# Seven products for three K pairs in the two output projections of a hybrid decoder trunk

## The chip, the cores and the metric

The kernel runs on one core of one Trainium2 chip. A core has TensorE (PE in the profile, with PEld for the loading of its weights), VectorE (DVE), ScalarE (ACT), GpSimd (POOL) and SyncE (SP, which here only issues DMAs). The metric is the device time of one execution in microseconds; a time is the median of several runs, and a profile is one more execution, taken by itself.

## The reference

The model is a trunk of two layers on 256 tokens of width 2048, in float32. Layer 0 has a Mamba-2 SSD mixer with an inner width of 4096, layer 1 differential attention with 16 heads; each mixer is followed by a SwiGLU FFN of width 5632. Every sub-layer has an RMSNorm before it and one behind it. Cut to what the change touches:

```python
for i in range(DEPTH):                       # DEPTH = 2
    h = rmsnorm(x, norm_mix_pre[i])
    if i % 2 == 0:
        m = ssd_mixer(h, ...)                # ends in: (y normed by group * norm_w) @ w_out   [256,4096]@[4096,2048]
    else:
        m = diff_attention(h, ...)           # ends in: (heads * subln) @ w_out                [256,2048]@[2048,2048]
    x = x + rmsnorm(m, norm_mix_post[i])
    h = rmsnorm(x, norm_ffn_pre[i])
    x = x + rmsnorm(swiglu(h, ...), norm_ffn_post[i])
```

The two products with `w_out` are the output projections of the title. In SSD, `norm_w` is a factor for each of the 4096 inner columns.

## The kernel before

**Products.** The 256 tokens are two tiles t = 0, 1 of 128. Weights stand in HBM as blocks of 128 x 4 x 512: 512 values of K in four rows of 128, and one column of 512 outputs. A block is split into a high part `hi` (ScalarE, rounded to fp32r) and a low part `lo` (VectorE, what is left), in `prep` (L126). The activations are split in the same way. A product of 128 K values is then three matmuls on TensorE, high by high, high by low and low by high, summed in PSUM. Two rows of 128 K values together are called a K pair (`kg` or `kp`).

**`mv`** (L177) makes one column of 512 outputs: for every K pair, 2 token tiles x 2 rows x 3 matmuls, with the second tile's products put off by `lag` steps. **`pair`** (L220) makes two columns of outputs at once. For a K pair that isn't in `seven` it does the same 24 matmuls as `mv` would for both columns. For one in `seven`, the 2 x 2 x 2 block product (token tile, K row, column) is made with seven products instead of eight, from sums of weight blocks (L261 to L263, VectorE) and "forms", sums of activation blocks that `make_form` (L817) prepares once. One more weight sum is made by a DMA that adds while it lands, issued on POOL (L247). Four of the products are summed over all three K pairs in PSUM tiles `cp`, and are combined once, behind the last of the three (L274 to L281). `done` then adds them to the accumulators. The FFNs use `pair` for nearly everything.

**The output projections** are made by `out_proj` (L679). Before the change they use `mv` for all columns. SSD: the first half of K (groups 0 to 3) is multiplied in the middle of the mixer (L786), all four columns; of the second half, column 0 is made at the mixer's end (L788), while its working pools are still open, and columns 1 to 3 after these are closed (L848). `norm_w` is put on the weights: `prep` gets `scale` and works in pieces of 128 x 512 (L137 and L138). Attention: one call, four columns (L1071).

**Behind a projection**, for each token tile: the row's sum of squares (`sums`, ScalarE), the product with the post-norm's row (POOL for columns 0 to 2, VectorE for column 3), then `norm_chain` (L642), which makes x, transposes it on TensorE and writes it, split, to `xT`, the input of the next sub-layer. The rows of the post-norm come from HBM through `pw(n)`, issued on SP; rows 0 and 2 share one buffer, so that row 2's fetch waits for the products with row 0.

**Order.** Work that is to run beside a product is put in a list with `later(k, fn)` and is emitted k steps further on (`tick`, L162), or when a product looks for it (`lookup`). A scheduler then orders the instructions of each engine and of each DMA queue, and places the waits; each engine runs its list in order. Weight blocks have three buffers (`raw`); after the mixer's pools close, `hi` and `lo` have four each.

Of the kernel before, what the change touches and what calls it, by code (L numbers as in the profile page):

```python
# [41 lines left out]
def trunk_kernel(ctx, tc, x_rows, x_cols, vec_cols, vec64, post_rows, lam_rows,  # L42
# [83 lines left out]
    def prep(raw, scale=None):  # L126
        i = seq[0]
        seq[0] += 1
        w = raw.shape[1]
        hi = hl[0].tile([P, w, 512], F32R, tag="hi", name=f"hi{i}")  # L130
        lo = hl[0].tile([P, w, 512], F32R, tag="lo", name=f"lo{i}")
        if scale is None:
            nc.scalar.copy(hi, raw)  # L133
            nc.vector.tensor_tensor(lo, raw, hi.bitcast(F32), op=ALU.subtract)  # L134
        else:
            for j in range(w):
                nc.scalar.activation(hi[:, j], raw[:, j], AF.Copy, scale=scale[j])  # L137
                nc.vector.scalar_tensor_tensor(lo[:, j], raw[:, j], scale[j], hi[:, j].bitcast(F32),  # L138
                                               op0=ALU.mult, op1=ALU.subtract)
        return hi, lo  # L140

    def halves(src, scale=None, raw=None):
# [3 lines left out]
        for e in range(0, 4, w):  # L146
            hi, lo = prep(raw[:, e:e + w], scale and scale[e:e + w])
            for k in range(0, w, 2):
                yield hi[:, k:k + 2], lo[:, k:k + 2]
# [27 lines left out]
    def mv(blocks, stat, evac, lag, scale=None, loaded=()):  # L177
# [14 lines left out]
        for b, src in enumerate(blocks):  # L192
            raw = loaded[b] if b < len(loaded) else None
            sc = scale(2 * b) + scale(2 * b + 1) if scale else None
            for i, (hi, lo) in enumerate(halves(src, sc, raw), 2 * b):
# [24 lines left out]
    def pair(blocks, stat, seven, form, done):  # L220
# [20 lines left out]
        for kp, src in enumerate(blocks):  # L241
# [3 lines left out]
            if kp in seven:  # L245

                nc.gpsimd.dma_start(raw[:, 0:1], src[0][:, 1:2], accum_op=ALU.add)  # L247
            if kp not in seven:
                hi, lo = prep(raw)
                for t in range(NT):  # L250
# [5 lines left out]
                    tick()  # L256
                continue
# [29 lines left out]
    def act_piece(src, name, scale=None):  # L287
# [6 lines left out]
        if scale is None:  # L294
            split(hi, lo, pt)
        else:
            nc.scalar.activation(hi, pt, AF.Copy, scale=scale)
            nc.vector.scalar_tensor_tensor(lo, pt, scale, hi.bitcast(F32), op0=ALU.mult, op1=ALU.subtract)
# [19 lines left out]
    rstd_bc = const.tile([P, S], F32, name="rstd_bc")  # L318

# [295 lines left out]
    def gate_group(g, t):  # L615
# [11 lines left out]
        def piece():  # L627
            ssd_act[(t, g)] = act_piece(yf, f"s{g}_{t}")
        later(4, piece)

# [48 lines left out]
    def out_proj(w, first, last, acts, kgs, step, final, lag, t512, pw, scale=None, ns=range(4), two={}, forms=None, md=None, mid=None):  # L679
# [20 lines left out]
        def row(t, e):  # L700
            if t not in ss4:
                ss4[t] = small.tile([P, 4], F32, tag="ss4", name="ss_m", bufs=3)
            if e not in summed[t]:
                summed[t].add(e)
                return sums(t, e)
# [3 lines left out]
        if last:  # L709
            pw(0)  # L710
            if two:
                pw(1)
        for n, seven in two.items():
            def done(t, c, ps, ss, n=n):
                y, op = ss[(t, c)]
                k = (t, n + 1 - c)
                nc.vector.tensor_tensor(y, ps, y, op=op)
# [6 lines left out]
                else:  # L724
# [3 lines left out]
                 lambda i, j, t: stat(kgs[i], j, t), [kgs.index(kg) for kg in seven], lambda i, f: form_of(lookup(forms, kgs[i]), f), done)  # L728
# [5 lines left out]
        for n in ns:  # L734
# [7 lines left out]
            def evac(t, ps, n=n):  # L742
# [11 lines left out]
                if n == 2:  # L754
                    p3 = small.tile([P, 1], F32, tag="ss1", name="p3", bufs=3)
                    nc.vector.tensor_reduce(p3, ss4[t][:, 0:3], axis=AX.X, op=ALU.add)
                    nc.vector.tensor_scalar(ss4[t][:, 0:1], p3, 1.0 / D, EPS, op0=ALU.mult, op1=ALU.add)
# [4 lines left out]
            mv([w[n, kg // 2] for kg in up[::2]], up_stat, evac, LAG if last and n == 3 else lag,  # L762
               (lambda i: [scale[:, 2 * up[i] + j:2 * up[i] + j + 1] for j in range(2)]) if scale is not None else None)

    for half in range(2):
# [19 lines left out]
        if half == 0:  # L785
            out_proj(w_so, True, False, ssd_act, list(range(8)), 0, False, 1, None, None, ssd_norm)  # L786

    out_proj(w_so, False, False, ssd_act, list(range(8, 16)), 0, False, 1, None, None, ssd_norm, ns=range(0, 1))  # L788
# [28 lines left out]
    def make_form(dct, key, stat, t512, keep=None):  # L817

        xf = t512("xf", (P, NT, 2, P))
        f = t512("f", (P, 4, P))  # L820
        for t in range(NT):
            for j in range(2):
                hi, lo = stat(key, j, t)
                nc.vector.tensor_tensor(xf[:, t, j], hi.bitcast(F32), lo.bitcast(F32), op=ALU.add)
        nc.vector.tensor_tensor(f[:, 0], xf[:, 1, 0], xf[:, 1, 1], op=ALU.subtract)
        nc.vector.tensor_tensor(f[:, 1], xf[:, 1, 0], xf[:, 0, 0], op=ALU.subtract)
        nc.vector.tensor_tensor(f[:, 2], xf[:, 0, 0], f[:, 0], op=ALU.subtract)
        nc.vector.tensor_tensor(f[:, 3], xf[:, 0, 1], f[:, 2], op=ALU.subtract)
        ff = dct[key] = xr_tile("ff", (P, 4, 2, P), F32R)
        split(ff[:, :, 0], ff[:, :, 1], f)  # L830
        if keep:
            nc.sync.dma_start(keep, ff.rearrange("p f h q -> p (f h q)").bitcast(F32))

    def form_of(ff, f):
        return ff[:, f, 0], ff[:, f, 1]

# [11 lines left out]
    out_proj(w_so, False, True, ssd_act, list(range(8, 16)), 0, False, LAG2, t512, load_post(0), ssd_norm, ns=range(1, 4))  # L848
# [285 lines left out]
```

## Time and profile before

| what | value |
|---|---|
| median of three runs | 2540.5 us (2540.33 to 2541.4) |
| the profiled execution's own time | 2541.16 us |
| its span, first to last instruction | 2539.4 us |
| granted TensorE clock, mean | 0.998 |
| weight loads of the SSD projection | 32 of 1024 KB, issued from 252.9 to 670.0 us |
| weight loads of the attention projection | 16 of 1024 KB, issued from 1690.2 to 1788.2 us |
| DMA | 536.16 MB, mean 211 GB/s |

The stretch of the second half of the SSD projection is about 612 to 698 us of the span, that of the attention projection about 1736 to 1816 us. In the page, a group's line gives its source line, engine, operation, tiles and shapes, its count, then its busy time and the mean ns of one, and then the idle time of the engine ahead of them with what ended it. The chain that ended last is followed back from the last instruction through what released each step, and shows which work sets the end. A matmul's recorded duration overlaps the next one's, so the pace of products is read from the start of one to the start of the next.

### The profile page before, as it was taken

Reading aid. Unit: us, or ns where it says so; the run is one execution under the profiler, and the core shown is the slowest. Engines: PE = TensorE matmul, PEld = TensorE weight load, DVE = VectorE, ACT = ScalarE, POOL = GpSimd, SP = SyncE. Lnnn points to the kernel's source line nnn. Section 1 sums busy time; section 2 is a strip of 40 time slices with the busy share of each in tenths; the row PEclk is TensorE's granted clock in tenths of the full one; section 3 lists DMA queues with packets and bytes.
Section 4 is the critical chain, followed back from the end, with each engine's and each line's share of the span. In section 5 each row is a group of like instructions: output and inputs, shape, how many; then the busy total and the mean of one; then the engine's idle time right before and its main releaser. Section 6 shows DMA issues by size and latency. Waiting matters only on the chain.

```text
span 2539.4 us, 31214 instructions
## 1 busy us (share of the span) xinstructions
PE 2517.3 (99%) x11866; PEld 2071.8 (82%) x11866; DVE 1901.7 (75%) x2274; ACT 1364.6 (54%) x1655; POOL 224.4 (9%) x214
## 2 busy tenths in 40 slices
PE   9999999999999999999999999999999999999998
PEld 7877888788888888888888888887888888888886
DVE  6777547777687888977887765566688889878985
ACT  5767546665565454544454654455655454535453
POOL 0121000110110000001001100001100000010002
PEclk9999999999999999999999999999999999999999
DMA  7545555554776776778677544544666966796673
GB/s 279 197 167 183 186 194 199 166 183 171 257 261 211 254 238 210 235 230 244 209 239 243 189 150 166 183 151 156 241 222 201 292 213 214 234 264 207 211 251 146
DMA packets 141366, 536.16 MB, mean 211 GB/s; under 512 B 14176, under 2 KB 30880, under 8 KB 114208
## 3 DMA queue, kind: packets, MB, share of 16 engines
q1 hardware_dynamic: 125584, 502.91, 57.3%
q0 software_dynamic: 15264, 30.94, 6.4%
q8 instruction: 93, 1.52, 0.2%
q14 instruction: 57, 0.47, 0.1%
q10 hardware_dynamic: 368, 0.32, 0.0%
HBM read 516.22 MB, written 17.89 MB: 210 GB/s over the span
## 4 chain that ended last, share of the span: by engine, by line
PE 91%; DVE 3%; issue 2%; ACT 2%; DMA 1%; POOL 0%; SPq 0%; DVEq 0%; ACTq 0%; POOLq 0%
PE acc L238 36%; PE acc L187 35%; PE cp L238 7%; PE acc L212 5%; PE acc L214 2%; DVE lo L134 2%; ACT hi L133 1%; PE sc L1010 1%; PE pt_f L291 1%; PE py L565 1%; DMA mt<-acum_d 1%; PE ptx L658 0%; PE po L1046 0%; PE pc L472 0%; PE pt_s L291 0%
## 5 line engine op out<-in xcount | busy, mean ns | idle before, releaser
L134 DVE TENSOR_TENSOR lo<-raw,hi 128x2048 fp32r<-128x2048 f32 (+2 forms) x451 | 848.2, 1888 | 363.0 <-ACT hi L133 362.2
L133 ACT CAST hi<-raw 128x2048 fp32r<-128x2048 f32 (+2 forms) x451 | 699.9, 1558 | 592.0 <-DVE raw L263 189.2
L238 PE MATMUL acc<-hi,xT 128*128 128x512 f32 x1840 | 589.0, 390 | 0.0
L187 PE MATMUL acc<-hi,xT 128*128 128x512 f32 x1792 | 586.1, 399 | 0.6 <-ACT hi L133 0.5
L238 PEld LDWEIGHTS acc<-hi,xT 128*128 128x128 f32 x1840 | 345.3, 188 | 71.5
L187 PEld LDWEIGHTS acc<-hi,xT 128*128 128x128 f32 x1792 | 335.8, 188 | 74.1 <-issue 4.9
L238 PE MATMUL acc<-lo,xT 128*128 128x512 f32 x920 | 358.1, 389 | 0.0
L187 PE MATMUL acc<-lo,xT 128*128 128x512 f32 x896 | 352.3, 394 | 2.6 <-DVE lo L134 2.6
L133 ACT CAST hi<-rawm 128x2048 fp32r<-128x2048 f32 (+1 forms) x115 | 207.8, 1807 | 173.7 <-DVE rawm L263 108.3
L134 DVE TENSOR_TENSOR lo<-rawm,hi 128x2048 fp32r<-128x2048 f32 (+1 forms) x115 | 248.1, 2157 | 70.2 <-ACT hi L133 66.1
L238 PEld LDWEIGHTS acc<-lo,xT 128*128 128x128 f32 x920 | 172.7, 188 | 35.7
L187 PEld LDWEIGHTS acc<-lo,xT 128*128 128x128 f32 x896 | 169.0, 189 | 40.2 <-DVE lo L134 5.5
L238 PE MATMUL acc<-hi,ah_f 128*128 128x512 f32 x468 | 183.1, 391 | 0.0
L238 PE MATMUL acc<-hi,al_f 128*128 128x512 f32 x468 | 182.2, 389 | 0.0
L238 PE MATMUL acc<-lo,ah_f 128*128 128x512 f32 x468 | 182.1, 389 | 0.0
L212 PE MATMUL acc<-xT,hi 128*128 128x512 f32 x512 | 180.4, 398 | 0.0
L238 PE MATMUL cp<-hi,ff 128*128 128x512 f32 x468 | 156.8, 389 | 0.0
L214 PE MATMUL acc<-xT,lo 128*128 128x256 f32 x512 | 143.0, 280 | 0.0
L138 DVE SCALAR_TENSOR_TENSOR lo<-raw,cols,hi 128x512 fp32r<-128x512 f32 x128 | 92.5, 769 | 56.6 <-ACT hi L137 56.3
L137 ACT ACTIVATE hi<-raw,cols 128x512 fp32r<-128x512 f32 x128 | 84.6, 715 | 59.4 <-PE acc L187 39.3
L212 PEld LDWEIGHTS acc<-xT,hi 128*128 128x128 f32 x512 | 96.1, 188 | 22.8
L238 PEld LDWEIGHTS acc<-hi,al_f 128*128 128x128 f32 x468 | 87.8, 188 | 18.3
(279 smaller groups left out, 3469.9 us busy)
## 6 DMA issues: line engine op xcount, KB each, us to landing
raw<-in_w_zxbc_dram SPq DMA_DIRECT2D x77, 1024.0 KB, 4.8
raw<-in_w_d_dram SPq DMA_DIRECT2D x98, 512.0 KB, 5.8
raw<-in_w_g_dram SPq DMA_DIRECT2D x96, 512.0 KB, 6.0
raw<-in_w_u_dram SPq DMA_DIRECT2D x96, 512.0 KB, 5.8
raw<-in_w_qkv_dram SPq DMA_DIRECT2D x48, 1024.0 KB, 4.7
raw<-in_w_so_dram SPq DMA_DIRECT2D x32, 1024.0 KB, 4.8
rawm<-in_w_g_dram SPq DMA_DIRECT2D x64, 512.0 KB, 5.9
rawm<-in_w_u_dram SPq DMA_DIRECT2D x64, 512.0 KB, 6.0
```

The lines of the kernel that those rows point to most:

```text
L133: nc.scalar.copy(hi, raw)
L134: nc.vector.tensor_tensor(lo, raw, hi.bitcast(F32), op=ALU.subtract)
L137: nc.scalar.activation(hi[:, j], raw[:, j], AF.Copy, scale=scale[j])
L138: nc.vector.scalar_tensor_tensor(lo[:, j], raw[:, j], scale[j], hi[:, j].bitcast(F32), op0=ALU.mult, op1=ALU.subtract)
L187: nc.tensor.matmul(acc[t], a, b[:, j], start=(i == 0 and j == 0 and q == 0), stop=(i == last and j == 1 and q == 2))
L212: nc.tensor.matmul(acc[ct], hi[:, j, cs], x.rearrange("p a s -> p (a s)"), start=(i == 0 and j == 0), stop=False)
L214: nc.tensor.matmul(acc[ct][:, :S], lo[:, j, cs], x[:, 0], start=False, stop=(i == last and j == 1))
L238: nc.tensor.matmul(acc[k], a, b, start=first and q == 0, stop=last and q == 2)
L291: nc.tensor.transpose(pt[:, j], src[:, j * P:(j + 1) * P], ident)
L565: nc.tensor.matmul(py[e * 64:(e + 1) * 64, a], xd[c][:, 2 * a + e], mts[c][:, 2 * a + e], start=True, stop=True)
L1010: nc.tensor.matmul(sc[c][:, h], qT[cp, h % 2, ts], kT[cp, h % 2, :nk * P], start=True, stop=True)
```

## The change

Both projections make columns 1 and 2 with `pair`, and three of its eight K pairs take seven products: K pairs 9, 11 and 13 of the second half in SSD, 1, 3 and 5 in attention. Column 0 and column 3 stay with `mv`. SSD's first half stays as it was, but for the scale.

- `norm_w` is no longer put on the weights. `act_piece` puts it on the activations, as a scale of each of the four 128-wide parts, so that `prep` loses its second branch.
- `make_form` and `form_of` move up, and `make_form` can be told where to put the form (`at`). The forms of the projections are put in `xT` (`idle_xT`), the mixer's input, which has had its last reader by then and isn't written again before `norm_chain`.
- `pair` gets `chip`: the sum that was made by a DMA issued on POOL is made by one more VectorE instruction on the loaded block.
- `pair` also gets `lead`, which stays 0, and its plain K pairs are written as a function; their order is the same.
- Attention's projection becomes two calls: column 0, then columns 1 and 2 with column 3.
- The rows' sums of squares and post-norm products move: row 0 at step 3 of the pair, the fetch of post-norm row 2 at step 4, rows 1 and 2 at steps 4 and 5 behind the pair. The sum over three rows is made when the third is there.
- `attention_group` is cut into functions for values, keys and the rest, called in the same order, and some helpers of `ffn` move out of it.

```diff
-    def prep(raw, scale=None):
+    def prep(raw):
...
-        if scale is None:
-            nc.scalar.copy(hi, raw)
-            nc.vector.tensor_tensor(lo, raw, hi.bitcast(F32), op=ALU.subtract)
-        else:
-            for j in range(w):
-                nc.scalar.activation(hi[:, j], raw[:, j], AF.Copy, scale=scale[j])
-                nc.vector.scalar_tensor_tensor(lo[:, j], raw[:, j], scale[j], hi[:, j].bitcast(F32),
-                                               op0=ALU.mult, op1=ALU.subtract)
+        nc.scalar.copy(hi, raw)
+        nc.vector.tensor_tensor(lo, raw, hi.bitcast(F32), op=ALU.subtract)
...
-    def pair(blocks, stat, seven, form, done):
+    def pair(blocks, stat, seven, form, done, lead=0, chip=False):
...
-            if kp in seven:
-
+            if kp in seven and chip:
+                nc.vector.tensor_tensor(raw[:, 0], raw[:, 0], raw[:, 1], op=ALU.add)
+            elif kp in seven:
                 nc.gpsimd.dma_start(raw[:, 0:1], src[0][:, 1:2], accum_op=ALU.add)
...
+        for sl in (slice(0, 4),) if scale.shape[1] == 1 else [slice(j, j + 1) for j in range(4)]:
+            sc = scale if scale.shape[1] == 1 else scale[:, sl]
+            nc.scalar.activation(hi[:, sl], pt[:, sl], AF.Copy, scale=sc)
+            nc.vector.scalar_tensor_tensor(lo[:, sl], pt[:, sl], sc, hi[:, sl].bitcast(F32),
+                                           op0=ALU.mult, op1=ALU.subtract)
...
+    def idle_xT(i):
+
+        return xT[i // 2][:, :, :, i % 2 * P:(i % 2 + 1) * P]
...
-            ssd_act[(t, g)] = act_piece(yf, f"s{g}_{t}")
+            ssd_act[(t, g)] = act_piece(yf, f"s{g}_{t}", scale=ssd_norm[:, 4 * g:4 * g + 4])
...
+                if len(summed[t]) == 3:
+                    p3 = small.tile([P, 1], F32, tag="ss1", name="p3", bufs=3)
+                    nc.vector.tensor_reduce(p3, ss4[t][:, 0:3], axis=AX.X, op=ALU.add)
+                    nc.vector.tensor_scalar(ss4[t][:, 0:1], p3, 1.0 / D, EPS, op0=ALU.mult, op1=ALU.add)
...
+            if 1 in two:
+
+                later(3, lambda: [row(t, 0) for t in range(NT)])
+                later(4, lambda: pw(2))
         for n, seven in two.items():
             def done(t, c, ps, ss, n=n):
                 y, op = ss[(t, c)]
                 k = (t, n + 1 - c)
+                if first and last:
+                    nc.vector.tensor_tensor(m[k], ps, y, op=op)
+                    return
...
+    sforms = {}
+    for k, kg in enumerate((9, 11, 13)):
+        later(2 + 2 * k, lambda k=k, kg=kg: make_form(
+            sforms, kg, act_stat(ssd_act), lambda name, shape: s2.tile(list(shape), F32, tag="t2", name=name), at=idle_xT(k)))
+    out_proj(w_so, False, False, ssd_act, list(range(8, 16)), 0, False, 1, None, None, ns=range(0, 1))
...
-    out_proj(w_so, False, True, ssd_act, list(range(8, 16)), 0, False, LAG2, t512, load_post(0), ssd_norm, ns=range(1, 4))
+
+    out_proj(w_so, False, True, ssd_act, list(range(8, 16)), 0, False, LAG2, t512, load_post(0), ns=(3,),
+             two={1: (9, 11, 13)}, forms=sforms)
...
-    out_proj(w_ao, True, True, att, list(range(8)), 2, False, LAG2, t512, load_post(2))
+    aforms = {}
+    for k, kg in enumerate((1, 3, 5)):
+        later(3 + 2 * k, lambda k=k, kg=kg: make_form(aforms, kg, act_stat(att), t512, at=idle_xT(k)))
+    out_proj(w_ao, True, False, att, list(range(8)), 2, False, LAG2, t512, None, ns=(0,))
+    out_proj(w_ao, True, True, att, list(range(8)), 2, False, LAG2, t512, load_post(2), ns=(3,),
+             two={1: (1, 3, 5)}, forms=aforms)
```

127 lines of the change are left out of this document (70 added, 57 removed).

## The prediction

> **What bounds the kernel now.** I read the page first: its head, the busy shares, the granted clock and the chain that ended last.
>
> ```profile
> span 2539.4 us, 31214 instructions
> PE 2517.3 (99%) x11866; PEld 2071.8 (82%) x11866; DVE 1901.7 (75%) x2274; ACT 1364.6 (54%) x1655; POOL 224.4 (9%) x214
> PEclk9999999999999999999999999999999999999999
> PE 91%; DVE 3%; issue 2%; ACT 2%; DMA 1%; POOL 0%; SPq 0%; DVEq 0%; ACTq 0%; POOLq 0%
> ```
>
> The reader is to see that TensorE (PE) has work in flight for 2517.3 of 2539.4 us and holds 91% of the chain. The page warns that a busy PE need not run at its peak, so the next views are the waits of PE alone (in all us, times, longest) and then the merged chain in order of time (start, us, what), at the two output projections and inside one FFN pair.
>
> ```profile
> PE acc L187 <- DVE lo L134: 2.6, 5, 1.3
> PE pc L472 <- ACT tk L478: 1.8, 1, 1.8
> PE ptx L658 <- DVE x L652: 1.5, 3, 0.7
> PE pwarm L328 <- POOL ones L317: 1.3, 1, 1.3
> PE px L552 <- DVE xg L460: 0.9, 2, 0.6
> PE ptx L658 <- issue: 0.7, 1, 0.7
> PE acc L187 <- ACT hi L133: 0.5, 1, 0.5
> ```
>
> ```profile
> 624.12 73.49 PE acc L187 x324
> ...
> 852.13 27.88 PE acc L238 x123
> ...
> 1758.99 53.50 PE acc L187 x235
> ```
>
> These are all waits of PE that the view names, 9.3 us in the whole program and none for a weight load. The chain crosses most of the SSD mixer's last projection as one unbroken run of 324 products: 73.49 / 324 = 0.2268 us from one to the next. The attention projection gives 53.50 / 235 = 0.2277, and a run inside a pair that already uses seven products gives 27.88 / 123 = 0.2267. So a product costs 0.2268 us in the form it has now and in the form it will have; the longer duration that the groups of the page show for a single matmul overlaps its neighbour and isn't the price.
>
> Last, the busy time of each engine in the two stretches (columns: length, PE, PEld, DVE, ACT, POOL, clock, DMA share, GB/s).
>
> ```profile
> 601.37:697.62 96.25, 96.25 (x429) 79.27 (x427) 62.17 (x90) 55.63 (x93) 10.63 (x9) 1.00 0.65 235
> 1736.00:1816.00 80.00, 79.30 (x366) 64.67 (x367) 42.66 (x51) 41.05 (x57) 14.83 (x9) 1.00 0.52 178
> ```
>
> PE is never idle in the first stretch and idle for 0.70 us in the second, at the full clock; VectorE (DVE) is busy 65% and 53%. TensorE's count of products sets the time here, and VectorE is the engine with least room behind it.
>
> **What the change removes on the path.** A column of one projection has 8 K pairs x 2 token tiles x 2 halves x 3 terms = 96 products, two columns 192. Three of the eight K pairs now take 7 x 3 = 21 products where they took 24: 5 x 24 + 3 x 21 = 183, so 9 fewer for each projection and 18 in all. 18 x 0.2268 = 4.08 us. Nothing else leaves TensorE, and nothing is added to it: forms and block sums are made on VectorE and ScalarE (ACT).
>
> The Trainium skill, "TensorE: Matmul & The Clock Gate", section "Back-to-back issue gap", gives about 131 ns for such a product in a sustained stream and about 216 ns for the gap of an isolated one. By these the saving would be an estimated 2.4 or 3.9 us; the 0.2268 us of this trace decides against both, and the sum above does not use them.
>
> **What it adds beside the path.** The rows by shape:
>
> ```profile
> L134 DVE TENSOR_TENSOR lo<-raw,hi 128x2048 fp32r<-128x2048 f32 x241 | 551.0, 2294 | 247.6 <-ACT hi L133 246.9
> L134 DVE TENSOR_TENSOR lo<-raw,hi 128x1024 fp32r<-128x1024 f32 x160 | 210.4, 1319 | 96.5 <-ACT hi L133 96.4
> L138 DVE SCALAR_TENSOR_TENSOR lo<-raw,cols,hi 128x512 fp32r<-128x512 f32 x128 | 92.5, 769 | 56.6 <-ACT hi L137 56.3
> L134 DVE TENSOR_TENSOR lo<-raw,hi 128x1536 fp32r<-128x1536 f32 x50 | 87.6, 1752 | 18.9 <-ACT hi L133 18.9
> L261 DVE TENSOR_TENSOR raw<-raw 128x512 f32<-128x512 f32 x50 | 34.5, 690 | 1.3
> L285 DVE TENSOR_TENSOR ff<-f,ff 128x512 fp32r<-128x512 f32 x18 | 12.3, 687 | 2.4 <-ACT ff L284 2.4
> L284 ACT CAST ff<-f 128x512 fp32r<-128x512 f32 x18 | 11.1, 619 | 13.4 <-PE cp L238 10.2 <-issue 3.0 <-DVE f L828 0.2
> L824 DVE TENSOR_TENSOR xf<-ah_f,al_f 128x128 f32<-128x128 f32 x48 | 11.5, 283 | 0.1
> L664 DVE SCALAR_TENSOR_TENSOR xT<-ptx,cols,xT 128x128 fp32r<-128x128 f32 x96 | 27.8, 345 | 5.3 <-ACT xT L663 5.1
> L285 DVE TENSOR_TENSOR al_s<-pt_s,ah_s 128x512 fp32r<-128x512 f32 x16 | 10.9, 683 | 2.2 <-ACT ah_s L284 2.2
> ```
>
> SSD scale: 128 scaled weight pieces at 0.769 become plain ones. In the last projection that frees 64 x 0.769 = 49.2 us of VectorE, and its old first column and fourth column come back as 8 x 1.319 + 4 x 2.294 = 19.7. The scale moves to 16 activation pieces, four 128x128 steps where one 128x512 stood: 4 x 0.345 - 0.683 = 0.7 us more for each, two or three of them in this stretch (2 us). The other projection of SSD only gets lighter, with PE unbroken there already, so it is costed at nothing.
>
> The pair: 5 x 2.294 for the plain K pairs; a seven-product one takes the new add on the chip and three block sums (4 x 0.690), the three-quarter low part (1.752) and the sums' low part (2.294), 6.81 us. Together 11.5 + 20.4 = 31.9. The end of a pair adds four combinations, and eight instructions in `done` replace four evacuations: 8 x 0.69 = 5.5. Three forms at 8 x 0.283 + 0.687 = 2.95 give 8.9. Sum: 62.2 - 49.2 + 19.7 + 2 + 31.9 + 5.5 + 8.9 = 81 us of VectorE in 96.25 - 9 x 0.2268 = 94.2. By busy time it still fits, behind TensorE. In attention the pair replaces 8 x 2.294 = 18.4: 42.7 - 18.4 + 31.9 + 5.5 + 8.9 = 71 in 78. The weight bytes and their number of landings per K pair stay those of the FFN pairs; the add that those give to a transfer is on VectorE here, so no POOL transfer is added.
>
> What can fail is order, not volume. A seven-product pair followed by a plain one, as an FFN pair of the same kernel runs it on VectorE:
>
> ```profile
> 881.61 1.76 DVE L134 TENSOR_TENSOR lo<-raw,hi 128x1536 fp32r<-128x1536 f32 x1 [2.71 <-ACT hi L133]
> 883.40 0.69 DVE L261 TENSOR_TENSOR raw<-raw 128x512 f32<-128x512 f32 x1
> ...
> 887.53 2.29 DVE L134 TENSOR_TENSOR lo<-raw,hi 128x2048 fp32r<-128x2048 f32 x1 [2.11 <-ACT hi L133]
> 889.74 2.29 DVE L134 TENSOR_TENSOR lo<-rawm,hi 128x2048 fp32r<-128x2048 f32 x1
> ```
>
> From 881.61 to 889.74 + 2.29 = 892.03 are 10.4 us, of which 2.11 is a wait for ScalarE that the next plain low part may fill (then 8.3). With the new add it is 11.1 (or 9.0), against (21 + 24) x 0.2268 = 10.2 on TensorE. So VectorE may lose up to 0.9 us in each of three rounds, 2.7 us for each projection, and needs a lead. What lead it has in SSD:
>
> ```profile
> 625.83 7.37 DVE L138 SCALAR_TENSOR_TENSOR lo<-raw,cols,hi 128x512 fp32r<-128x512 f32 x11
> 633.74 0.69 DVE L748 TENSOR_TENSOR m<-m,acc 128x512 f32<-128x512 f32 x1 [0.54 <-PE acc L187]
> ```
>
> Column 0 ends on TensorE at about 633.7, and by 633.2 VectorE has finished eight pieces of column 1, two blocks or 48 x 0.2268 = 10.9 us of products. The forms (8.9), two pieces (1.4) less the lighter column 0 (16 x 0.769 - 8 x 1.319 = 1.8) take 8.5 of it if no idle time of VectorE takes them up: a lead of 2.4 us or more, against up to 2.7 us lost. The two are about even. The lower bound is no stall; the upper is 2.7 - 2.4 = 0.3 plus three waits of a form for its own ScalarE step, 0.62 each, 2.2 us. I take 0.5 us, nearer to the lower end, because VectorE has idle time to give before column 1: the 56.6 us ahead of L138 are 0.44 for each of its 128 pieces, 7 us in the 16 of column 0. In attention VectorE prepares up to four blocks ahead, and I cost the same loss at nothing; if that cover were gone it would be the 2.7 us.
>
> **A wait added.** `pw(2)`, the third post-norm row, is now fetched after the row-0 products on POOL, early in the pair; it is issued on SP, and weight loads of later K pairs stand behind it there, which ScalarE, VectorE and then TensorE wait for.
>
> ```profile
> 648.64 1.29 POOL L688 TENSOR_TENSOR m<-m,wpost 128x512 f32<-128x512 f32 x1 [27.41 <-DMA wpost<-in_post_rows_dram]
> 655.71 3.30 POOL L688 TENSOR_TENSOR m<-m,wpost 128x512 f32<-128x512 f32 x2 [5.78 <-ACT junk L302]
> SPq L806 <- POOL m L688: 28.2, 6, 9.4
> raw<-in_w_d_dram SPq DMA_DIRECT2D x98, 512.0 KB, 5.8
> 633.22 0.33 SPq L123 DMA_DIRECT2D raw<-in_w_so_dram  x1
> 636.45 1.75 SPq L841 DMA_DIRECT2D x<-in_x_rows_dram  x4
> ```
>
> SP already waits like this 28.2 us in all in the program, up to 9.4 at once, and no PE wait above is for a weight load. So zero is taken. The upper bound is in the rivals.
>
> The Trainium skill, "SBUF — State Buffer", section "Who interferes with whom", speaks against moving the sums to VectorE: its instructions with two SBUF inputs keep out a GpSimd instruction that reads SBUF. The trace agrees in kind (1.29 us alone above, a mean of 1.65 in the pair of 3.30); it would make the wait on SP longer, and gives no term of the sum.
>
> **The sum.** -4.08 + 0.5 = -3.6 us. The profiled execution took 2541.16 (span 2539.4), so 2537.6 on its scale; against the median of 2540.5 it is **2536.9 us**. A measurement of this kernel can tell about 0.2%, 5.1 us, from no change, and the whole saving is below that.
>
> **Rivals.**
>
> *VectorE becomes the bound in SSD.* The lead is short by 0.3 us, the forms' three waits are added and no wait of ScalarE is filled, and what is lost in the first round delays the buffers of the next: a loss of 2 to 5 us, so 2538.4 to 2541.4. For it: 81 of 94 us, and a lead nearly used up. Against it: the FFN pairs run at 10.4 against 10.2 with PE unbroken. 15%.
>
> *The SP queue starves the pair: slower than before.* POOL's row-0 products end at about 648.64 + 3.3 = 651.9, since the row they need lands no earlier. K pair 4 is due on TensorE two plain and two seven-product pairs after column 0: 633.7 + 90 x 0.2268 = 654.1. If its load stands behind `pw(2)`, it lands at 651.9 + 5.8 = 657.7; with a high part (1.9, the 2.11 above less its signals) and a low part (2.3) it is ready at 661.9, 7.8 us late, and the time is 2540.5 - 4.1 + 7.8 = 2544.2. If K pair 2 is held too, due at 643.9, it is 18 us late: 2554. The mechanism makes the kernel slower from a loss of 4.08 us, which is K pair 4's load issued after about 648.2. For it: the calls stand in this order in the code. Against it: the trace shows SP with the loads of columns 1 and 2 (the first of column 2 at 633.22) ahead of the fetch of x (636.45), which stands before them in the code. 12%, of which 7 beyond 2545.6.
>
> *The norm chain gains too.* PE's idle time at the ends of the projections:
>
> ```profile
> 690.00:720.00 30.00, 28.80 (x140) 22.84 (x139) 24.98 (x48) 20.08 (x45) 3.08 (x2) 1.00 0.81 285
> ```
>
> 1.2 us here and 0.7 in attention. Rows 1 and 2 are squared earlier now; if that closes both gaps the time is 2540.5 - 4.08 - 1.9 = 2534.5. Against: the last steps before the transposes are the same. 13%.
>
> *It doesn't do what it says:* all loss is placed so that no product is saved on the path. Since PE is unbroken, I see no place for it, and give it no chance beyond the first rival's upper end.
>
> **How the numbers follow.** The forecast has 60% (2535.6 to 2538.4, its own range), the rivals 15, 12 and 13%. The range of 2535.0 to 2542.0 holds the forecast, the VectorE case and the near end of the norm-chain case, and leaves out the rest of that and the SP case. Faster by over 0.2% (under 2535.4) is the norm-chain case, 0.13; slower by over 0.2% (over 2545.6) is the far part of the SP case, 0.07; within 0.2%, 0.80.
>
> **What would show it.** 11848 products on PE; runs in the chain at 0.2268 in both projections; waits of PE for `lo` near the start of the SSD pair show the second term; a PE wait after an SP wait on POOL shows the slow rival. The forecast is wrong if PE idles over 2 us in either pair, or if the product's pace differs.

## The result and the profile after

The changed kernel takes **2562.4 us** (median; 2561.9 to 2562.9) beside 2540.6 us for the kernel before on the same chip. The ratio is 1.0084, with a 95% interval of 1.007 to 1.0098. The forecast was 2536.9 us, with a range up to 2542.0: the direction is wrong, and so is the range.

First the page of the changed kernel: its head, the busy shares, and the chain that ended last by engine.

```profile
span 2560.7 us, 31277 instructions
PE 2523.2 (99%) x11848; PEld 2072.3 (81%) x11848; DVE 1944.9 (76%) x2346; ACT 1366.6 (53%) x1637; POOL 228.4 (9%) x214
PE 64%; DVE 5%; issue 3%; ACT 2%; DMA 1%; POOL 0%; SPq 0%; DVEq 0%; ACTq 0%; POOLq 0%
```

The 18 products are gone (11866 to 11848), and the busy share of PE still reads 99%. But PE's share of the chain fell from 91% to 64%. A share of busy time didn't show the loss; the share of the chain did.

To place it I cut the span at four marks that both traces have: the last gate `zth` of SSD and the first transpose `ptx` of the norm after it, the last `qk` scaling of attention and the first `ptx` after that. Between them lie the tail of the mixer, column 0, the pair and column 3 of each projection. The windows of before, then of after, with a stretch of 20 us in attention's column 0 for each, and a stretch early in the kernel (length; busy time and records of PE, PEld, DVE, ACT and POOL; granted clock; DMA share; GB/s):

```profile
615.94:698.33 82.39, 81.68 (x365) 67.28 (x364) 54.25 (x79) 48.15 (x81) 10.09 (x8) 1.00 0.67 241
1724.42:1815.67 91.25, 90.56 (x416) 72.75 (x415) 49.37 (x67) 46.73 (x75) 14.83 (x9) 1.00 0.48 166
140.00:145.00 5.00, 5.00 (x22) 3.77 (x21) 4.35 (x9) 2.79 (x6) 0.00 (x0) 1.00 0.63 210
...
1750.00:1770.00 20.00, 20.00 (x102) 16.43 (x101) 9.86 (x14) 10.28 (x13) 6.11 (x4) 1.00 0.34 120
```

```profile
618.60:708.94 90.34, 82.10 (x354) 64.56 (x353) 70.21 (x90) 46.71 (x53) 14.49 (x8) 1.00 0.63 220
1735.50:1837.14 101.64, 93.56 (x406) 73.81 (x404) 73.53 (x117) 51.04 (x78) 15.48 (x9) 0.95 0.42 150
140.00:145.00 5.00, 5.00 (x15) 3.61 (x14) 3.18 (x6) 2.35 (x5) 0.00 (x0) 0.68 0.64 208
1760.00:1780.00 20.00, 14.23 (x53) 11.01 (x54) 13.55 (x35) 7.38 (x13) 2.35 (x3) 0.74 0.18 66
```

SSD's projection grew by 7.95 us and attention's by 10.39, where each should have shrunk by 2.04. Together they lost 18.3 + 4.1 = 22.4 us against their products. Ahead of SSD's mark the span is 2.66 us longer (615.94 to 618.60); most of this first appears at 140 us, where this one profile shows a granted clock of 0.68. Five microseconds at 0.68 are an estimated 1.6 us lost. The fifteen other kernels with the scale moved are 0.8 to 1.5 us late at that mark, each in one profile. Everything else differs by 0.3 us: 7.95 + 10.39 + 2.66 + 0.30 = 21.3, the difference of the spans.

The waits of PE (in all us, times, longest) and a piece of VectorE's order in attention (start, us) show who is late:

```profile
PE pt_o L297 <- DVE ob L1096: 4.3, 2, 3.5
PE acc L181 <- DVE lo L133: 4.1, 7, 1.4
...
PE cp L233 <- ACT hi L132: 1.9, 2, 1.2
PE acc L233 <- ACT hi L132: 1.9, 3, 1.0
PE pp L1079 <- DVE e L1069: 1.9, 1, 1.9
```

```profile
1757.77 0.69 DVE L269 TENSOR_TENSOR raw<-raw 128x512 f32<-128x512 f32 x1
1758.37 0.89 DVE L341 TENSOR_TENSOR xf<-ah_o,al_o 128x128 f32<-128x128 f32 x4
...
1761.10 2.29 DVE L133 TENSOR_TENSOR lo<-raw,hi 128x2048 fp32r<-128x2048 f32 x1
1763.31 0.29 DVE L344 TENSOR_TENSOR f<-xf,f 128x128 f32<-128x128 f32 x1
1763.51 0.68 DVE L1094 TENSOR_REDUCE sso<-ob 128x4 f32<-128x512 f32 x1
...
1765.77 0.69 DVE L1096 TENSOR_TENSOR ob<-po,rs_o 128x512 f32<-128x512 f32 x1 [0.90 <-POOL rs_o L93]
1766.38 0.68 DVE L291 TENSOR_TENSOR xT<-f,xT 128x512 fp32r<-128x512 f32 x1
```

PE has no wait of 0.3 us or more for a form's own tile. VectorE works its list in order. In it, work for the pair (block sums L269, form additions L341 and L344, the pair's low part L133) stands between the softmax and the last `ob` steps, which PE waits for. PE had 53 records in 20 us there, at a mean granted clock of 0.74, where before had 102 at 1.00.

In SSD's pair the chain passes over SP as well: the fetch of the third row, which waited for POOL, then a weight load, then VectorE.

```profile
656.75 0.33 SPq L857
...
658.08 7.03 DMA raw<-in_w_so_dram
...
666.71 3.96 DVE lo L133 x2
```

On TensorE the loss in SSD divides like this: from the last product of the gate to the first of the pair are 24.5 us (617.00 to 641.51), where a kernel with plain pairs (e8_plain below) takes 21.6; the pair itself takes 48.4 us, where 183 products at 0.2267 are 41.5. So about 2.9 us go to column 0 and 6.9 to the pair.

### The profile page after: what moved, and what is told of

It reads as the page before. It is cut to its first block, busy times and chain, and to the rows that moved or that the text cites. A ratio compares the mean times of both kernels' runs of the same rounds, so it can differ in the third digit from the quotient of the medians.

```text
span 2560.7 us, 31277 instructions
## 1 busy us (share of the span) xinstructions
PE 2523.2 (99%) x11848; PEld 2072.3 (81%) x11848; DVE 1944.9 (76%) x2346; ACT 1366.6 (53%) x1637; POOL 228.4 (9%) x214
## 4 chain that ended last, share of the span: by engine, by line
PE 64%; DVE 5%; issue 3%; ACT 2%; DMA 1%; POOL 0%; SPq 0%; DVEq 0%; ACTq 0%; POOLq 0%
PE acc L233 35%; PE acc L181 12%; PE cp L233 7%; PE acc L205 5%; DVE lo L133 3%; PE acc L207 2%; ACT hi L132 2%; PE sc L1052 1%; PE pt_f L297 1%; DMA raw<-in_w_d_dram 1%; PE ptx L698 0%; PE po L1088 0%; DVE raw L267 0%; DVE raw L268 0%; DMA raw<-in_w_so_dram 0%
## 5 line engine op out<-in xcount | busy, mean ns | idle before, releaser
L133 DVE TENSOR_TENSOR lo<-raw,hi 128x2048 fp32r<-128x2048 f32 (+2 forms) x509 | 938.4, 1851 | 389.5 <-ACT hi L132 386.0
L132 ACT CAST hi<-raw 128x2048 fp32r<-128x2048 f32 (+2 forms) x509 | 773.2, 1526 | 635.9 <-DVE raw L269 218.5
L133 DVE TENSOR_TENSOR lo<-rawm,hi 128x2048 fp32r<-128x2048 f32 (+1 forms) x115 | 247.6, 2153 | 71.0 <-ACT hi L132 67.1
L233 PEld LDWEIGHTS acc<-hi,al_f 128*128 128x128 f32 x468 | 87.8, 188 | 18.3
L233 PEld LDWEIGHTS cp<-hi,ff 128*128 128x128 f32 x468 | 87.9, 188 | 18.1
L233 PEld LDWEIGHTS acc<-hi,ah_f 128*128 128x128 f32 x468 | 87.9, 188 | 17.9
```

What stands on the lines that cost most here:

```text
L233: nc.tensor.matmul(acc[k], a, b, start=first and q == 0, stop=last and q == 2)
```

## The experiments

The expectations name these theories. **V**: VectorE does the pair's extra work ahead of steps on which PE waits, or makes the pair itself late; later V was split into **F** (the forms do it) and **S** (the block sums and the chain of a seven-product K pair do it). **Q**: SP waits for POOL before it fetches the third row, with weight loads behind it. **O**: a seven-product K pair stands too early in the pair. **P**: VectorE and POOL slow each other. The last two columns are the two stretches marked above, from one profile each; the count of products alone gives 80.35 and 89.21 for three seven-product K pairs. How far one profile can be trusted shows in after, e4_attlate and e2_ssd: VectorE, SP and POOL carry the same list in SSD there, and the stretch took 90.34, 91.54 and 92.30 us. So in a stretch that stalls, a difference under 2 us tells nothing by itself. Stretches with plain products agree within 0.2 us.

| kernel | median us | ratio to before (95%) | SSD | attention |
|---|---|---|---|---|
| before | 2540.6 | 1 | 82.39 | 91.25 |
| after | 2562.4 | 1.0084 (1.0070, 1.0098) | 90.34 | 101.64 |
| e1_scale | 2541.7 | 1.0002 (0.9992, 1.0011) | 82.21 | 91.26 |
| e2_ssd | 2551.1 | 1.0037 (1.0024, 1.0051) | 92.30 | 91.23 |
| e3_row2 | 2559.1 | 1.0073 (1.0056, 1.0089) | 88.18 | 101.15 |
| e4_attlate | 2554.4 | 1.0052 (1.0037, 1.0067) | 91.54 | 94.45 |
| e5_rowpool | 2559.9 | 1.0076 (1.0061, 1.0091) | 90.26 | 101.49 |
| e6_late | 2550.8 | 1.0039 (1.0024, 1.0053) | 85.04 | 95.85 |
| e7_latedma | 2549.8 | 1.0036 (1.0023, 1.0049) | 88.16 | 94.61 |
| e8_plain | 2542.1 | 1.0007 (0.9998, 1.0016) | 82.32 | 91.43 |
| e9_noform | 2546.6 | 1.0025 (1.0015, 1.0034) | 82.71 | 96.25 |
| e10_late_noform | 2542.8 | 1.0008 (0.9998, 1.0017) | 81.85 | 91.83 |
| e11_nosum | 2540.0 | 0.9999 (0.9989, 1.0008) | 80.95 | 90.92 |
| e12_one | 2541.0 | 1.0003 (0.9994, 1.0012) | 81.54 | 91.00 |
| e13_noform_rowpool | 2544.3 | 1.0014 (1.0005, 1.0023) | 80.24 | 96.33 |
| e14_late_noform_sp | 2547.5 | 1.0025 (1.0015, 1.0036) | 82.74 | 95.99 |
| e15_poolform | 2562.2 | 1.0084 (1.0068, 1.0101) | 90.54 | 101.95 |

**e1_scale**: the kernel before, with only the scale of SSD moved from the weight pieces to the activation pieces.

```diff
-            ssd_act[(t, g)] = act_piece(yf, f"s{g}_{t}")
+            ssd_act[(t, g)] = act_piece(yf, f"s{g}_{t}", scale=ssd_norm[:, 4 * g:4 * g + 4])
```

> The kernel before, with only the norm factor moved from the weights to the activation pieces. The prediction's view (TensorE unbroken there): 2540.5 us, within 1. The rival view, from the trace after, where the cores' first stretch ends 2.3 us later from 140 us on with a granted clock of 0.68 in one 5 us stretch: 2542 to 2544 if the small steps of the pieces cause it, 2540.5 if it comes with the rest of the change.

2541.7 beside 2541.2 us in its own batch: the moved scale costs nothing that can be told in the time.

**e2_ssd**: the change without its attention part.

```diff
-    out_proj(w_ao, True, False, att, list(range(8)), 2, False, LAG2, t512, None, ns=(0,))
-    out_proj(w_ao, True, True, att, list(range(8)), 2, False, LAG2, t512, load_post(2), ns=(3,),
-             two={1: (1, 3, 5)}, forms=aforms)
+    out_proj(w_ao, True, True, att, list(range(8)), 2, False, LAG2, t512, load_post(2))
```

> The change without the attention part (its projection by four plain columns). If the two projections lose independently, the trace after puts 10.6 us of loss ahead of the first norm chain, so 2551 us; if the attention part is innocent, 2562.

2551.1, as forecast for two independent losses: about half of the loss belongs to each projection. They can be studied apart.

**e3_row2**: the fetch of the third row issued ten steps later.

```diff
-                later(4, lambda: pw(2))
+                later(14, lambda: pw(2))
```

> The change with the fetch of post-norm row 2 ten steps later, so that no weight load of the pair stands behind a row product of POOL on SP. Theory Q (the SP queue starves the pair): the pairs lose 5.2 us in SSD and 3.7 in attention over what they save, so 2553 to 2557 us. Theory V (VectorE's list: forms and block sums stand ahead of the mixers' last steps): within 1.5 us of 2562.4.

2559.1, between the forecasts of Q and V. In SSD the fetch moved behind five loads and not two, and the stretch is 2.2 us below the shortest of the three above; another 1.9 us lie ahead of the first mark, before any such fetch. In attention SP's order stayed as it was, and the edit didn't test it.

**e4_attlate**: attention's seven-product K pairs at places 2, 4, 6 of the eight, not 1, 3, 5 (counted from 0), and its forms eight steps later.

```diff
-        later(3 + 2 * k, lambda k=k, kg=kg: make_form(aforms, kg, act_stat(att), t512, at=idle_xT(k)))
+        later(11 + 2 * k, lambda k=k, kg=kg: make_form(aforms, kg, act_stat(att), t512, at=idle_xT(k)))
-    out_proj(w_ao, True, True, att, list(range(8)), 2, ...
+    out_proj(w_ao, True, True, att, [0, 2, 1, 4, 3, 6, 5, 7], 2, ...
```

> The change with attention's forms eight steps later, and the seven-product K pairs at places 2, 4, 6 of the pair instead of 1, 3, 5. Theory V: attention's column 0 loses 9.2 us to forms and block sums ahead of the softmax, so about 2553 us. Theory Q: column 0's loss is no matter of the forms, and at most 3.7 us come back, 2558 to 2562.

2554.4, near V's 2553, and attention's stretch is 7.2 us shorter: the loss in its column 0 is one of order, and the instructions are the same. The pair behind it stayed long.

**e5_rowpool**: the third row fetched on POOL's own queue, so that SP doesn't wait.

```diff
-                nc.sync.dma_start(w[n], post_rows[ix, ...
+                (nc.gpsimd if n == 2 else nc.sync).dma_start(w[n], post_rows[ix, ...
```

> The change with every fetch of post-norm row 2 issued on POOL, behind its own row products, so that SP never waits for POOL there (in the runs before, SP waited 21 to 23 us for it beside attention's pair). Theory Q: the late loads are what both pairs lose, so -4 in SSD and -3 or more in attention, 2553 to 2556 us. Theory V: VectorE's chain of high part, low part, sums and low part is what the pairs wait for, so no more than run e3_row2 gave in SSD and nothing in attention, 2558 to 2560.

2559.9, as V had it: neither stretch moves by more than 0.2 us. The wait on POOL is gone from SP's queue in the pair, but beside attention's pair SP now waits up to 20.9 us at once for a low part on VectorE. Of the 2.5 us less than the change took, 1.67 lie ahead of the first mark (616.93 and 618.60), before any such fetch.

**e6_late**: e5_rowpool with the order of e4_attlate in both projections, and SSD's forms made behind column 0 too.

```diff
+        later((1, 4, 8)[k], lambda k=k, kg=kg: make_form(sforms, kg, act_stat(ssd_act), t512, at=idle_xT(k)))
-    out_proj(w_so, False, True, ssd_act, list(range(8, 16)), 0, ...
+    out_proj(w_so, False, True, ssd_act, [8, 10, 9, 12, 11, 14, 13, 15], 0, ...
-        later(3 + 2 * k, ... make_form(aforms, ...
+        later((11, 13, 16)[k], ... make_form(aforms, ...
```

> As e5_rowpool, and both projections make their forms behind column 0, with the seven-product K pairs at places 2, 4, 6. Theory V: the 4.8 us of SSD's column 0 and the 8.5 of attention's come back, and the two plain K pairs ahead give VectorE a lead; what stays is its 11.1 us for each 10.2 of TensorE plus the forms, 5 us in a pair at most: 2543 to 2548. Theory Q alone: as e5_rowpool, less the 8 us that run e4_attlate gave.

2550.8, above V's forecast. Column 0 of SSD takes its old time again (21.6 us on TensorE, 615.67 to 637.29), but both pairs are still long. VectorE's timeline at the first addition of column 0 in the changed kernel, and then in e6_late with a part of its pair:

```profile
641.11 0.68 DVE L800 TENSOR_TENSOR m<-m,acc 128x512 f32<-128x512 f32 x1
```

```profile
634.80 0.68 DVE L800 TENSOR_TENSOR m<-m,acc 128x512 f32<-128x512 f32 x1
...
643.54 4.49 DVE L133 TENSOR_TENSOR lo<-raw,hi 128x2048 fp32r<-128x2048 f32 x2 [1.38 <-ACT hi L132]
647.95 3.07 DVE L341 TENSOR_TENSOR xf<-ah_s,al_s 128x128 f32<-128x128 f32 x4
...
656.02 1.75 DVE L133 TENSOR_TENSOR lo<-raw,hi 128x1536 fp32r<-128x1536 f32 x1
```

From the last gate (618.60, 617.16; before 615.94) to this addition are 22.5, 17.6 and, before, 17.8 us. The changed kernel's VectorE reaches it 4.7 us later than before; TensorE itself lost 2.9 us in column 0. In e6_late about 8 us of forms stand between two low parts, and the four additions that take 0.89 us elsewhere took 3.07 beside a row product on POOL. In the whole stretch of SSD these are the waits of PE for the pair, both for a form itself:

```profile
PE acc L233 <- ACT xT L290: 2.2, 1, 2.2
...
PE acc L233 <- DVE xT L291: 0.2, 1, 0.2
```

Behind the first, some nine products follow each other at 0.427 us and not 0.2267: the clock fell, to a mean of 0.89 from 647 to 657 us. The row product on POOL:

```profile
648.14 2.73 POOL L728 TENSOR_TENSOR m<-m,wpost 128x512 f32<-128x512 f32 x2 [26.91 <-DMA raw<-in_w_so_dram]
```

**e7_latedma**: e6_late, with the first block sum made by the load itself (an adding DMA on POOL, as in the FFN pairs).

```diff
-                 ..., lambda i, f: form_of(lookup(forms, kgs[i]), f), done, chip=1 in two)
+                 ..., lambda i, f: form_of(lookup(forms, kgs[i]), f), done)
```

> e6_late with the first block sum made by a DMA that adds as it lands, as the FFNs do. Theory V: 0.7 us less on VectorE for each of six K pairs, 2 to 4 us faster than e6_late. If the load is what is late, the added transfer behind another makes it slower.

2549.8: no difference from e6_late that can be told, and not the 2 to 4 us of V. In SSD the wait for the form grew to 5.1 us and the stretch by 3.1.

**e8_plain**: e5_rowpool with no seven-product K pair: the same pair with 24 products for each K pair, no forms, sums or combinations.

```diff
-             two={1: (9, 11, 13)}, forms=sforms)
+             two={1: ()})
-             two={1: (1, 3, 5)}, forms=aforms)
+             two={1: ()})
```

> As e5_rowpool, but no K pair takes seven products: columns 1 and 2 run in pairs with all 24 products each, with no forms, no block sums and no combinations. Theory V: pairs cost nothing by themselves, 2540 to 2542 us. Theory Q or the pair's form itself: still several us above, since loads, rows and buffers are as in the change.

2542.1: columns 1 and 2 as a pair, and the rows' new order with the third row on POOL's queue, are innocent. What is left is VectorE's work for the seven-product K pairs, and the next kernels take it apart.

**e9_noform**: the change with the forms left out. **e10_late_noform**: e6_late with the forms left out.

```diff
-        later(..., lambda k=k, kg=kg: make_form(sforms, kg, ...))
+        sforms[kg] = idle_xT(k)
-        later(..., lambda k=k, kg=kg: make_form(aforms, kg, ...))
+        aforms[kg] = idle_xT(k)
```

> The changed kernel with the six forms left out (the seven-product K pairs read whatever lies in the mixer input's place; sums, products and combinations are as in the change). Theory F (the forms are what VectorE does in the mixers' last steps): column 0 takes its old 17.7 us in SSD and 34.2 us in attention, so 4.7 + 8.8 us come back, and some of the 5.2 + 5.6 us lost in the pairs: 2546 to 2549. Theory S (the block sums and low parts of the pair, run ahead of their turn, stand in the way in attention): SSD's column 0 comes back (4.7), attention's by less than half: 2553 to 2558. Theory Q (SP's queue): nothing of the pairs' loss comes back, as in F for column 0.

> e6_late with the six forms left out. e6_late lost 4.9 us in the SSD pair and 5.1 in attention's against the pairs' products. Theory F: the forms (8.9 us of VectorE for each pair) made the pairs late; without them the pairs take 62.6 and 50.3 us or a little over, and the kernel 2538 to 2541. Theory S: the chain of a seven-product K pair on VectorE itself (high part, low part, sums, high part, low part: about 11 us for a seven and a plain one, where TensorE has 10.2) is the loss; the forms only add to it: 2545 to 2549.

2546.6, as F had it, and 2542.8, between the forecasts of F and S. Without the forms 15.8 us of 21.8 come back where the change makes them, and 8.0 us where e6_late makes them (in the stretches 7.6 + 5.4 and 3.2 + 4.0; of the rest of the 15.8, 1.85 us lie ahead of the first mark). So the forms are the largest part, and not all. Leaving a form out also takes away its step on ScalarE and the wait for the form itself; the trace of the changed kernel has no such wait, so there their place on VectorE is the likelier cost. What stays in attention in e9_noform has another cause, by its chain:

```profile
1769.43 2.79 POOL m L728
...
1772.23 0.33 SPq L854
...
1772.67 4.68 DMA raw<-in_w_ao_dram
...
1777.38 0.60 DVE raw L242
```

A row product on POOL, then SP's fetch, then a weight load, then VectorE: the rival that the prediction gave 12%, there for SSD alone.

**e11_nosum**: e10_late_noform with the four block sums of each seven-product K pair left out too.

```diff
-            nc.vector.tensor_tensor(raw[:, 2], raw[:, 2], raw[:, 0], op=ALU.add)
-            nc.vector.tensor_tensor(raw[:, 3], raw[:, 3], raw[:, 2], op=ALU.add)
-            nc.vector.tensor_tensor(raw[:, 1], raw[:, 2], raw[:, 1], op=ALU.subtract)
...
```

> e10_late_noform with the four block sums of each seven-product K pair of the two projections left out too (the second high and low parts are made of the unsummed blocks). VectorE gets 2.76 us less per such K pair, 8.3 us per pair, and the second high part no longer waits for the first low part and the sums. Theory S: what e10 still lost in the pairs goes, and the kernel takes 2537 to 2540, about 4 us under the kernel before. Theory F: the same as e10, within 1 us. If both pairs still lose here, the cost lies in the buffers of the second high and low parts, a cause that neither names.

2540.0, at the edge of S's forecast and not F's: the sums cost 2.8 us in the median (0.9 us in each stretch, by one profile; the rest lies outside them). So S is a part of the loss too. Even with forms and sums free, this order only reaches the time before. Its stretches keep 0.6 and 1.7 us above the count of products, and I didn't take that apart.

**e12_one**: a single seven-product K pair for each projection, the fifth of the eight, its form behind column 0, and the row on POOL's queue.

```diff
-             two={1: (9, 11, 13)}, forms=sforms)
+             two={1: (12,)}, forms=sforms)
-             two={1: (1, 3, 5)}, forms=aforms)
+             two={1: (4,)}, forms=aforms)
```

> One seven-product K pair per projection instead of three, the fifth of the eight, its form made behind column 0 and the third row's fetch on POOL's queue. It saves 6 products, 1.36 us. Theory S and theory F: with four plain K pairs ahead of it and three behind, VectorE can take the 3.8 us more of this K pair and the 3.0 us of a form from its lead: 2539.5 to 2542, no different from the kernel before, and the only form of the change that doesn't lose. If it takes over 2544, a single one already costs more than it saves, and the lead of VectorE in these pairs is under some 3 us.

2541.0, no different from before, but both stretches are shorter (by 0.85 and 0.25 us; three products are 0.68). Its chain in SSD:

```profile
625.33 12.29 PE acc L181 x54
637.62 21.76 PE acc L233 x96
659.38 0.68 PE cp L233 x3
660.06 1.36 PE acc L233 x6
661.42 2.04 PE cp L233 x9
663.46 17.00 PE acc L233 x75
680.46 17.68 PE acc L181 x78
```

This is what the forecast promised for three: TensorE unbroken at 21.76 / 96 = 0.2267 us, through the seven-product K pair too.

**e13_noform_rowpool** (e9_noform with e5_rowpool's edit) and **e14_late_noform_sp** (e10_late_noform without it) part the two edits between e9 and e10.

> e9_noform (the six forms left out, seven-product K pairs at places 1, 3, 5) with the third row fetched on POOL's queue and not on SP's. e9_noform to e10_late_noform gave 3.8 us back, and two edits lie between them: the queue of the fetch, and the places 2, 4, 6. Theory Q (SP waits for POOL's row products with weight loads behind it; in e9_noform the chain that ended last runs over that wait in attention): nearly all of the 3.8 us comes back, 2542.5 to 2543.5, and attention's projection takes about 92 us in place of 96.3. Theory O (a seven-product K pair at place 1 meets VectorE and ScalarE without a lead): under 1 us comes back, 2545.5 to 2547.

> e10_late_noform (forms left out, places 2, 4, 6) with the third row's fetch back on SP's queue. Theory Q: the 3.8 us go again, 2546 to 2547. Theory O: no change against e10_late_noform, 2542.5 to 2543.5. If this one and e13_noform_rowpool both lie near 2543, either edit alone cures the wait: the fetch holds a load back only where that load is due early.

2544.3, between the forecasts of Q and O, and 2547.5, Q's. With the forms left out, the four cases are:

| row fetched on | sevens at places | SSD | attention |
|---|---|---|---|
| SP (e9) | 1, 3, 5 | 82.71 | 96.25 |
| POOL (e13) | 1, 3, 5 | 80.24 | 96.33 |
| SP (e14) | 2, 4, 6 | 82.74 | 95.99 |
| POOL (e10) | 2, 4, 6 | 81.85 | 91.83 |

```diff
-                (nc.gpsimd if n == 2 else nc.sync).dma_start(w[n], post_rows[ix, ...
+                nc.sync.dma_start(w[n], post_rows[ix, ...
```

The diff is that of e14 to e10; e13 to e9 is its reverse. In SSD the queue alone costs 2.5 us, and without it the stretch takes its count of products (80.35). In attention either wait alone holds some 4 us, and only both edits together free them. The profile of e13_noform_rowpool took 1.4 us more than its median, so its wait may be nearer 3. That second wait is in column 0: with the places 1, 3, 5, PE waits 1.1 us for `e` and 1.2 for `al_o`, both of VectorE, in e13_noform_rowpool. The medians agree with the table for the queue: 2.3 us from e9 to e13, 4.6 from e14 to e10. What SSD keeps in e10 lies behind the pair: PE waits 1.1 us for low parts in column 3. Q put its gain in the wrong projection for e13_noform_rowpool, and O is no cause that stands by itself.

**e15_poolform**: e6_late with the eight small additions of each form on POOL.

```diff
+        eng = nc.vector if at is None else nc.gpsimd
-                nc.vector.tensor_tensor(xf[:, t, j], hi.bitcast(F32), lo.bitcast(F32), op=ALU.add)
+                eng.tensor_tensor(xf[:, t, j], hi.bitcast(F32), lo.bitcast(F32), op=ALU.add)
...
```

> e6_late with the eight small additions of each form on POOL in place of VectorE (the low part of a form stays on VectorE, 0.69 us). Theory F: what costs is VectorE's time, so most of what leaving the forms out gave back (2550.8 to 2542.8) comes back here too: 2543.5 to 2546. Rival (theory P): VectorE and POOL slow each other where both read two operands from on-chip memory (the row product on POOL 2.79 us beside VectorE where it took 1.29 alone, four form additions on VectorE 3.07 beside POOL where they took 0.89), so the forms come late or VectorE loses as much as it gains: 2549 or more.

2562.2, 11.4 us more than e6_late, in P's range. POOL in SSD's pair, and the first wait of PE:

```profile
637.33 3.98 POOL L342 TENSOR_TENSOR xf<-ah_s,al_s 128x128 f32<-128x128 f32 x4 [16.37 <-DMA raw<-in_w_so_dram]
...
644.10 6.26 POOL L342 TENSOR_TENSOR xf<-ah_s,al_s 128x128 f32<-128x128 f32 x4
...
655.27 2.17 POOL L342 TENSOR_TENSOR xf<-ah_s,al_s 128x128 f32<-128x128 f32 x4
```

```profile
PE cp L233 <- ACT hi L132: 5.5, 2, 5.0
```

The same four additions took 2.17 us where VectorE was busy for about half of them, and 3.98 and 6.26 where it was busy nearly throughout; a single one took 0.45 beside an idle VectorE and 0.91 beside a busy one. That is P's slowing. Even undisturbed, 0.45 is more than the 0.28 of VectorE, so part of the cost is POOL's own pace. By the chain the low part of the last form waits on VectorE for POOL, at 661.65, with the block sums behind it, then the second high part, for which PE waits 5.0 us. No kernel here beats the one before.

## Why the prediction was wrong, step by step

- **18 products at 0.2268 us: right.** The count is 11848 and the pace in unbroken runs stays at 0.2267 (e12_one). The saving shows where nothing holds the pair up: SSD in e13_noform_rowpool takes 80.24 us against 80.35 by count.
- **The moved scale at nothing: right** (e1_scale, +0.5 us, no difference that can be told). A price of about 1 us isn't ruled out: the first mark is 0.8 us late or more in every kernel that has it.
- **VectorE's volume fits: right, and not the question.** It is busy 70.21 of 90.34 us in SSD's stretch and 73.53 of 101.64 in attention's. The chain runs over it none the less.
- **The forms (8.9 us for each projection), hidden in VectorE's idle time: this step failed**, and it is the main one. The prediction set a lead of 2.4 us against 2.7 us lost, and took the forms for filler that uses idle time. In a list that is worked in order they are no filler: they stand ahead of the mixer's last steps. They cost 13.0 us in the two stretches (after to e9_noform). Moved behind column 0, they stand among the pair's low parts, come late themselves, and still cost 7.2 (e6_late to e10_late_noform).
- **Attention's loss costed at nothing, because VectorE prepares four blocks ahead: failed.** The largest loss is there, 10.39 + 2.04 = 12.4 us. The lead was VectorE's lead over a plain column behind a finished mixer; here column 0 itself still waited for the mixer. The line that could have told it was the order of VectorE's instructions before `ob`, which I hadn't read.
- **The wait of SP for POOL at zero: failed, the rival was real.** Its price was given as up to 7.8 us in SSD. With the forms gone it is 2.5 us in SSD at the early places (0.9 at the late ones) and some 4 us in attention at the late places. In the changed kernel the sign that the prediction named is there, in SSD's pair (the chain over SPq L857 above), but the cure moves neither stretch (e5_rowpool): without that wait VectorE's own work holds the pair as long.
- **"VectorE becomes the bound in SSD", 15%: the right mechanism, mis-sized and in one place of two.** I priced it at 2 to 5 us from the rounds of the pair; SSD lost 10.0 against its count, about 6.9 of them in the pair and 2.9 in column 0, which the rival left out.
- **The norm chain's gain:** didn't come; the wait before the transposes is 0.71 us in SSD as before, and 0.61 for 0.70 in attention.

The sum of the loss in the stretches, 22.4 us, in this order of taking away (in another order the parts differ: the forms cost 7.2 when moved first): forms 13.0 (after to e9); SP's queue in SSD 2.5 (to e13); queue and early place together in attention 4.4 (e9 to e10); the rest 2.5, all of it in attention, where the sums are 0.9 (e10 to e11). What stays open is that 1.7 us, and whether the low clock at 140 us belongs to every execution of the changed kernel: its one profile shows it, and those of the other kernels don't.

## What to carry to other kernels

Before work is put into an engine's idle time, read which instructions of that engine's list it will stand in front of and who waits for them: idle time in a sum of volumes is no lead. When a cure for one wait moves nothing, the wait can still be real: take away the larger one and test again (e5 against e13, and either edit in attention against both). And read PE's share of the chain beside its busy share.

## What the runs showed of the hardware that I had not expected

POOL's one-column power step in SSD's tail, in after and then in e9_noform, where VectorE has no form additions:

```profile
623.01 3.21 POOL L93 TENSOR_TENSOR rs_g<-ms_g,mhalf 128x1 f32<-128x1 f32 x1 [5.07 <-DVE ms_g L90]
```

```profile
620.27 0.55 POOL L93 TENSOR_TENSOR rs_g<-ms_g,mhalf 128x1 f32<-128x1 f32 x1 [4.18 <-DVE ms_g L90]
```

It took 3.21 us beside the forms and 0.55 without them, on the way to the last activation piece; PE waited 1.0 us there. The two other traces with the same list in SSD, e2_ssd and e4_attlate, have 3.21 too. The Trainium skill, "SBUF — State Buffer", section "Who interferes with whom", says that a VectorE instruction with two SBUF inputs contends with a GpSimd instruction that reads SBUF; these rows and e15_poolform agree, and the 3.07 us for 0.89 in e6_late show that VectorE pays too.

The granted clock makes a stall longer than its wait. In attention's column 0 the five-microsecond windows of after read:

```profile
1765.00:1770.00 5.00, 2.56 (x12) 1.26 (x10) 4.23 (x14) 1.84 (x4) 0.73 (x1) 1.00 0.59 226
1770.00:1775.00 5.00, 2.72 (x9) 2.36 (x10) 3.97 (x12) 1.24 (x2) 1.12 (x1) 0.64 0.00 0
1775.00:1780.00 5.00, 5.00 (x17) 3.94 (x16) 0.48 (x1) 1.31 (x3) 0.12 (x1) 0.68 0.00 0
1780.00:1785.00 5.00, 5.00 (x24) 4.13 (x23) 1.34 (x1) 3.77 (x5) 1.85 (x2) 1.00 0.00 0
```

After a stretch with PE about half idle, PE is busy again from 1775, but at a clock of 0.68 and with 17 records in 5 us where the next window, at full clock, has 24: a product every 0.427 us and not 0.2267. Over the whole of attention's stretch PE is idle 7.4 us more than before, and busy 5.0 us more than 9 products fewer would have it (93.56 against 90.56 - 2.04), at a mean clock of 0.95. So about 5 of that stretch's 12.4 us are longer products; by the mean clock, most of them are its fall (an estimate from these figures: 5% of 101.64).
